# Modulation vectors: partition sums by VectorE with a 32x32 turn, and gate rows spread by repeating loads from DRAM

## The chip, the cores and the metric

The kernel runs on one core of a Trainium2 chip. The metric is the device time of one execution in microseconds (us). A core has five engines that run their own instruction streams side by side and wait for each other by semaphores: TensorE (PE in the profile, its weight loads PEld), VectorE (DVE), ScalarE (ACT), GpSimd (POOL) and SyncE (SP), which here mainly issues DMA transfers.

## The reference

One layer for 256 context rows and 2048 latent rows of width 1024. Two vectors (one for context rows, one for latent rows) go through a linear map and give six vectors of 1024 each, the modulation:

```python
def adaln(cvec, w_mod, b_mod):
    m = jax.nn.silu(cvec) @ w_mod + b_mod
    return jnp.split(m[:, None, :], 6, axis=-1)

sh1, sc1, g1, sh2, sc2, g2 = adaln(c, w_mod[l], b_mod[l])      # the same for c_ctx
h = rms_norm(xs, norm1_g[l]) * (1 + sc1) + sh1
q, k, v, f = project(h, w_in[l], q_norm_g[l], k_norm_g[l])     # one product, RMS norm of q and k
...                                                            # attention, Fourier mixing, w_out
xs = xs + g1 * mix
h = rms_norm(xs, norm2_g[l]) * (1 + sc2) + sh2
xs = xs + g2 * sq_relu_mlp(h, w1[l], w2[l])
```

The gates g1 and g2 multiply whole rows: each of the 1024 columns has its own factor, the same for all rows of a kind.

## The kernel before

The 2304 rows are 18 tiles of 128 rows; the context tiles and the latent tiles go through the same stages, one after the other: projection (to about 480 us), Fourier mixing (to about 600), attention, output projection (from about 1285), the first MLP product, the last product (from 2227 to the end).

**Projection.** `proj(i, g)` makes group g (0 to 3: q, k, v, Fourier) of tile i: 24 matmuls of 128x512 into one PSUM bank `pj{i}_{g}`, of which there are four in rotation. Each product is made of three, of high and low halves (lines 87 to 89). For q and k, ScalarE squares the bank (`sq{i}_0`, `sq{i}_1`, L250), VectorE sums the squares (`qss`, L251) and scales them (L254), GpSimd raises them to the power −1/2 (`qrs`, L255), and VectorE multiplies the bank by that (`qn`, L268). After that multiplication the bank is free for the next tile. The rotation of axial positions follows on VectorE (`qo`, `qt`, lines 293 to 303), then a transpose on TensorE (`ptqT`, `ptkT`, for the last tiles `ptqkT`, L310). The Fourier group is read by two operations of `f_post` on VectorE (`fo`, L387, and `fh`, L388); only then is its bank free.

The tiles 1 to 16 are one loop whose instructions a scheduler orders on each engine; tile 17 and all that follows is in an order written by hand. The engines keep the order that results, so an instruction that waits holds up all behind it on its engine.

**Modulation.** The weights of the modulation come in pieces of 1024x512 (a group; 12 in all). Groups 4 to 11 are made inside the loop, one in each odd turn i: SP loads the piece (`wm`), and `mod_group_v` accumulates on VectorE, for either of the two vectors, eight multiples of [128x512] tiles into `macc` (L164, L166). What is left is the sum over the 128 partitions. TensorE does it: eight fp32 matmuls of a 128x128 block of `macc` with a column of ones give `pm`, 128 results in 128 partitions each (L168), and a VectorE addition of the bias puts them into `modc` (L142), which holds the modulation with the column index in the partitions.

**Gates.** The multiplication by a gate needs its 1024 values along a row, the same in all 128 partitions. `mk_gate` makes half of such a tile: four fp32 matmuls take a column of `modc`, repeated 128 times, against the identity (`pg`, L180), and ScalarE copies the result (L181). It is called four times for `g1` in the output projection and four times for `g2` in the first turn of the last stage.

Of the kernel before, what the change touches and what calls it, by code (L numbers as in the profile page):

```python
# [11 lines left out]
F32 = mybir.dt.float32  # L12
F32R = mybir.dt.float32r
AF = mybir.ActivationFunctionType
ALU = mybir.AluOpType
AX = mybir.AxisListType
# [3 lines left out]
P = 128  # L20
D = 1024
# [20 lines left out]
def body(tc, a, out):  # L42
    nc = tc.nc
    ctx = ExitStack()
    with ctx:
# [6 lines left out]
        def scratch(name, shape):  # L52
            return dram.tile(shape, F32, tag=name, name=name)
# [9 lines left out]
        four = scratch("four", [512, NT])  # L63
        xnew = [scratch(f"xnew{i}", [P, D]) for i in range(NT // P)]
        HB = NT // 2
        hop = [[scratch(f"hd{p}_{b}", [P, 4, 384]) for b in range(3)] for p in range(8)]
        tsum = [scratch(f"tsum{k}", [P, 3, 512]) for k in range(16)]
        sop = [[scratch(f"sd{p}_{b}", [P, 16, 384]) for b in range(3)] for p in range(8)]

        ident = cst("ident", [P, P])  # L70
# [3 lines left out]
        ones = cst("ones", [P, 1])  # L74
# [65 lines left out]
        def mod_bias(gi, pm):  # L140
            b = cols[:, 32 + gi * 4:32 + gi * 4 + 4].unsqueeze(2).to_broadcast([P, 4, 2])
            nc.vector.tensor_add(modc[:, gi * 4:gi * 4 + 4, :], pm, b)  # L142
# [10 lines left out]
                nc.tensor.transpose(pm[:, j, :], r[0:2, j * P:(j + 1) * P], ident[0:2, 0:2])  # L153
            mod_bias(gi, pm)

        def mod_group_v(t2, pps, gi, w):

            pm = pps.tile([P, 4, 2], F32, tag="pm", name=f"pm{gi}")
            for s in range(2):
                acc = t2(f"macc{gi}_{s}")  # L160
                for k in range(KD):
                    wk, sc = w[k // 2][:, k % 2, :], cols[:, 8 * s + k:8 * s + k + 1]
                    if k == 0:
                        nc.vector.tensor_scalar_mul(acc, wk, sc)  # L164
                    else:
                        nc.vector.scalar_tensor_tensor(acc, wk, sc, acc, op0=ALU.mult, op1=ALU.add)  # L166
                for j in range(4):
                    nc.tensor.matmul(pm[:, j, s:s + 1], acc[:, j * P:(j + 1) * P], ones, start=True, stop=True)  # L168
            mod_bias(gi, pm)

        def mk_scale(dst, c0, gcol):
            nc.vector.tensor_scalar_add(dst, modc[:, c0:c0 + KD, :], 1.0)
            nc.vector.tensor_mul(dst, dst, cols[:, gcol:gcol + KD].unsqueeze(2).to_broadcast([P, KD, 2]))

        def mk_gate(pps, dst, c0, s, halves=(0, 1)):
            for hf in halves:
                pg = pps.tile([P, 512], F32, tag="pg", name=f"pg{c0}_{s}_{hf}", bufs=1)
                for j in range(4):
                    col = modc[:, c0 + hf * 4 + j, s:s + 1]
                    nc.tensor.matmul(pg[:, j * P:(j + 1) * P], col.to_broadcast([P, P]), ident, start=True, stop=True)  # L180
                nc.scalar.copy(dst[:, hf * 512:hf * 512 + 512], pg)  # L181

        def norm(pool, xt, nm, dst=None):

# [24 lines left out]
        with ExitStack() as c1:  # L209
# [6 lines left out]
            def t2(nm):  # L216
                return p1.tile([P, 512], F32, tag="t2", name=nm, bufs=6)
# [198 lines left out]
            with tc.manual_schedule():  # L416
# [108 lines left out]
                v_split(1, 0, vo0, "v0")  # L525
                load(3)
            wm, LAST = None, N1 - 1
            for i in range(1, LAST):
                mg = 3 + (i + 1) // 2
                if i >= 2 + N1 // 2 - 1:  # L530
                    f_load(i)
                    if i > 2 + N1 // 2 - 1:
                        f_rev(i - 1)
                if i % 2 and mg < 12:
                    wm = mod_load(po, mg)
                if i > 1:
                    norm(p1, X[i + 1], f"a{i + 1}")
                    proj(i, 0)
                transposed(i + 1)
                if 1 < i < N1 - 2:  # L540
                    load(i + 2)
                squares(i, 0)
                if i > 1:
                    proj(i, 1)
                qk_T(i - 1)
                squares(i, 1)
                proj(i, 2)
                qk_post(i)
                v_post(i)
                proj(i, 3)  # L550
                f_post(i)
                if i % 2 and mg < 12:
                    mod_group_v(t2, pps, mg, wm)
                if i in (4, 6, 8, 10):
                    cache_tile((i - 4) // 2)
            mk_scale(scale2, 32, 88)
# [853 lines left out]
        with c3o, ExitStack() as c4, ExitStack() as c4x, ExitStack() as c4w:  # L1410
# [22 lines left out]
            def x_load(i):  # L1433
                src = a["x_prompt"][0][i * P:i * P + P] if i < 2 else a["x_sample"][0][i * P - NP:i * P - NP + P]
                if i == LAST:
                    XT[i] = [f32(ms2s.tile([P, 2, 384], F32R, tag="sh", name=f"xo{i}_{hf}", bufs=2)).rearrange("p a b -> p (a b)")[:, 0:512]
                             for hf in range(2)]
                    for hf in range(2):
                        nc.sync.dma_start(XT[i][hf], src[:, hf * 512:hf * 512 + 512])
                else:  # L1440
                    XT[i] = tx.tile([P, D], F32, tag="x", name=f"xo{i}", bufs=3)
                    nc.sync.dma_start(XT[i], src)
# [73 lines left out]
            with tc.manual_schedule():  # L1516
                N4 = len(seq)
                s0, s1, s2 = seq[:3]
                mix_load(s1)
                x_load(s0)  # L1520
                x_load(s1)
                w_split(1, 0, 1)
                mix(s0)
                w_split(1, 1, 4)
                out_mm(s0, 1, 0, 2)
                for fn in LASTO[:2]:
                    fn()
                w_split(1, 4)
                out_mm(s0, 1, 2, 4)
                for fn in LASTO[2:]:  # L1530
                    fn()
                mix(s1)
                out_mm(s0, 1, 4)
                mk_gate(pp, g1[1], 16, 1, (1,))
                w_split(0)
                kv_even.close()
                ms1 = ctx.enter_context(tc.tile_pool(name="m_s1", bufs=2, side="right"))
                ms2s = ctx.enter_context(tc.tile_pool(name="m_s2s", bufs=2, side="right", reuse_waits="tile"))
                mix_load(s2)
                x_load(s2)  # L1540
                out_mm(s1, 1)
                mk_gate(pp, g1[0], 16, 0, (1,))
                out_post(s0, 1)
                out_mm(s0, 0)
                mk_gate(pp, g1[1], 16, 1, (0,))
                out_post(s1, 1)
                mix(s2)
                out_post(s0, 0)
                x_store(s0)
                x_norm(s0)  # L1550
                mix_load(seq[3])
                x_load(seq[3])
                out_mm(s1, 0)
                mk_gate(pp, g1[0], 16, 0, (0,))
                out_post(s1, 0)
                x_store(s1)
                x_norm(s1)
                finish(s0)
                for n, i in enumerate(seq[2:], 2):
                    out_mm(i, 0)  # L1560
                    if n < N4 - 1:
                        mix(seq[n + 1])
                    if n < N4 - 2:
                        mix_load(seq[n + 2])
                        x_load(seq[n + 2])
                    if n == N4 - 1:
                        c4w.close()
                        c4x.close()
                        ms2 = ctx.enter_context(tc.tile_pool(name="m_s2", bufs=2, side="right", reuse_waits="tile"))
                        c5r = ExitStack()  # L1570
                        hpa = c5r.enter_context(tc.tile_pool(name="m_ha", bufs=1, side="right", reuse_waits="tile"))
                    if n == N4 - 1:
                        mlp_ahead(0)
                    out_post(i, 0)
                    if n == N4 - 1:
                        mlp_ahead(3)
                    finish(seq[n - 1])
                    out_mm(i, 1)
                    if n == N4 - 1:
                        mlp_ahead(1)  # L1580
                    out_post(i, 1)
                    x_store(i)
                    if n < N4 - 1:
                        x_norm(i)
                    if n == N4 - 7:
                        w_load(0)
                    if n in (N4 - 6, N4 - 5, N4 - 4):
                        h_load(0, ORDER[n - N4 + 6])
                    if n == N4 - 3:
                        w_ahead()  # L1590
                        w_load(1)
# [250 lines left out]
        with ExitStack() as c6:  # L1842
# [62 lines left out]
            with tc.manual_schedule():  # L1905
                pend, NM, loaded, KS = None, 7 * 24, 4, []
                for i in range(7):
                    for b in range(3):
                        ps = [pp.tile([P, 512], F32, tag="ps", name=f"ps{i}_{b}_{j}", bufs=6) for j in range(3)]
                        for k in range(16):  # L1910
# [19 lines left out]
                            if (i, b) == (6, 2) and 9 <= k < 12:  # L1930
# [2 lines left out]
                                u = U3[6 + j]  # L1933
                                nc.vector.tensor_mul(u, u, g2[0][:, 0:512])
                                nc.vector.tensor_add(u, u, X[j])
                            if i == 0 and b == 1 and k in (2, 6, 10, 14):
                                s, hf = divmod(k // 4, 2)
                                mk_gate(pp, g2[s], 40, s, (hf,))
                            KS.append((k, SO[m], TO[n]))
                            if i == 6 and b == 2 and 12 <= k < 15:  # L1940
                                continue
# [84 lines left out]
```

## Time and profile before

| | |
|---|---|
| time, median of 3 runs (lowest, highest) | 2917.53 us (2917.14, 2917.74) |
| profiled execution: span from the first to the last instruction | 2919.2 us |
| TensorE busy | 2884.2 us, 99% |
| VectorE, ScalarE, GpSimd busy | 2018.9, 1564.1, 1044.6 us |
| mean granted TensorE clock | 0.998 |
| `pm` matmuls (L168) | 128 records, 107.3 to 456.2 us |
| `pg` matmuls (L180) | 64 records, 1293.5 to 2284.1 us |

The profiled execution has no other time of its own than its span, which is 1.7 us above the median of the timed runs. A row of a timeline gives start, duration, engine, line, operation, output <- inputs, shapes and count, and in brackets the idle time of the engine just before it with what ended it. A row of a window gives its length, then the busy time of PE, PEld, DVE, ACT and POOL with the number of instructions, the granted clock of TensorE (1.00 is full speed), the DMA share and GB/s. A row of the waits gives who waited for whom, the total, the number of waits and the longest.

### The profile page before, as it was taken

What the parts mean: (1) busy time and instruction counts of PE and PEld (TensorE: products, weight loads), DVE (VectorE), ACT (ScalarE), POOL (GpSimd) and SP (SyncE); (2) the same over time, 40 slices, a digit from 0 to 9 for tenths busy, and PEclk for the clock granted to TensorE, in tenths of its full rate; (3) what the DMA queues carried; (4) which work ended last, traced back from release to release, by engine and by line L of the source; (5) the groups of instructions that cost most, each with busy time, mean ns of one, the idle gap of its engine ahead of it and who ended that gap; (6) DMA issues with size and microseconds to landing.
All of it is one profiled execution on the core that took longest, in us unless ns stands there. A gap on an engine that the chain in (4) does not pass through costs nothing.

```text
span 2919.2 us, 43814 instructions
## 1 busy us (share of the span) xinstructions
PE 2884.2 (99%) x15425; PEld 2505.5 (86%) x15425; DVE 2018.9 (69%) x3401; ACT 1564.1 (54%) x3524; POOL 1044.6 (36%) x849
## 2 busy tenths in 40 slices
PE   8999999999999999999999999999999999999999
PEld 4888888688888888888889999999998888888887
DVE  6666777888998988964468778778775344345554
ACT  4333323688998989964356566556554322232221
POOL 1111113199898999952213333333332000000000
PEclk9999999999999999999999999999999999999999
DMA  7777878611121201217776677676656354445663
GB/s 280 198 203 189 224 199 254 230 67 71 44 104 47 109 28 46 89 54 214 215 247 214 221 238 234 221 239 221 222 189 235 124 197 153 135 142 174 205 206 108
DMA packets 394415, 495.59 MB, mean 170 GB/s; under 512 B 26403, under 2 KB 307056, under 8 KB 391122
## 3 DMA queue, kind: packets, MB, share of 16 engines
q1 hardware_dynamic: 386560, 477.63, 51.3%
q0 software_dynamic: 2992, 7.28, 0.8%
q10 hardware_dynamic: 4642, 7.88, 0.8%
q8 instruction: 122, 2.00, 0.3%
q14 instruction: 99, 0.81, 0.1%
HBM read 315.20 MB, written 179.57 MB: 169 GB/s over the span
## 4 chain that ended last, share of the span: by engine, by line
PE 91%; DMA 3%; ACT 2%; DVE 2%; issue 1%; POOL 1%; SPq 0%; ACTq 0%; POOLq 0%; DVEq 0%
PE Ss L969 10%; PE ps L87 8%; PE ps L88 8%; PE ps L89 8%; PE pts L1024 5%; PE pj L89 4%; PE pj L87 4%; PE pj L88 4%; PE po L89 4%; PE po L87 4%; PE po L88 4%; PE pA L1634 2%; PE pA L1635 2%; PE pB L1634 2%; PE pB L1635 2%; PE pB L1636 2%
## 5 line engine op out<-in xcount | busy, mean ns | idle before, releaser
L974 DVE TENSOR_REDUCE mxs<-Ss 128x1 f32<-128x512 f32 x636 | 413.2, 685 | 65.5 <-PE Ss L969 52.7
L1309 DVE TENSOR_TENSOR sl<-sr,sh 128x768 fp32r<-128x768 f32 x168 | 161.7, 964 | 340.0 <-ACT sh L1308 339.5
L1009 POOL TENSOR_TENSOR P0s<-P0s,P1s 128x1024 f32<-128x1024 f32 (+2 forms) x128 | 377.2, 2947 | 10.7
L1308 ACT CAST sh<-sr 128x768 fp32r<-128x768 f32 x168 | 140.1, 835 | 424.9 <-PE ps L88 424.9
L1676 POOL TENSOR_TENSOR gs<-g,g 128x384 f32<-128x384 f32 x48 | 69.7, 1452 | 469.6 <-ACT g L1646 400.9
L993 ACT ACTIVATE P1s<-Ss,mxs 128x512 f32<-128x512 f32 x318 | 215.4, 695 | 35.6 <-DVE mxs L977 34.2
L87 PE MATMUL pj<-wh,hh 128*128 128x512 f32 x576 | 229.5, 399 | 0.7 <-ACT fo L381 0.7
L88 PE MATMUL ps<-tlT,sh 128*128 128x512 f32 x585 | 229.3, 392 | 0.0
L87 PE MATMUL ps<-thT,sh 128*128 128x512 f32 x585 | 229.2, 392 | 0.0
L88 PE MATMUL pj<-wl,hh 128*128 128x512 f32 x576 | 227.7, 395 | 0.5 <-DVE wl L503 0.5
L89 PE MATMUL ps<-thT,sl 128*128 128x512 f32 x585 | 227.7, 389 | 0.0
L89 PE MATMUL pj<-wh,hl 128*128 128x512 f32 x576 | 226.7, 394 | 0.0
L993 ACT ACTIVATE P0s<-Ss,mxs 128x512 f32<-128x512 f32 x318 | 214.3, 691 | 4.3 <-DVE mxs L977 3.7
L969 PE MATMUL Ss<-KS1s,Qs 128*128 128x512 f32 x636 | 196.3, 420 | 5.7 <-ACT P0s L993 3.1
L969 PE MATMUL Ss<-KS0s,Qs 128*128 128x512 f32 x636 | 196.5, 421 | 2.4 <-ACT P1s L993 2.4
L1024 PEld LDWEIGHTS pts<-ident,P0s 128*128 128x128 f32 x1280 | 158.2, 140 | 42.9 <-ACT ahs L1031 3.1
L1024 PE MATMUL pts<-ident,P0s 128*128 128x128 f32 x1280 | 191.2, 273 | 0.7 <-ACT P1s L993 0.7
L1645 ACT ACTIVATE g<-uz 128x384 f32<-128x384 f32 x144 | 75.8, 527 | 201.0 <-DVE uz L1668 175.0
L1008 POOL TENSOR_SCALAR P1s<-P1s,tots 128x1024 f32<-128x1024 f32 (+2 forms) x128 | 172.1, 1345 | 5.7
L1036 DVE TENSOR_TENSOR als<-pts,ahs 128x512 fp32r<-128x512 f32 x256 | 165.8, 681 | 6.9 <-ACT ahs L1031 6.6
L87 PE MATMUL ps<-ophT,sh 128*128 128x512 f32 x423 | 165.9, 392 | 1.1 <-DVE uz L1668 1.1
L89 PE MATMUL ps<-ophT,sl 128*128 128x512 f32 x423 | 165.7, 392 | 0.0
(640 smaller groups left out, 8202.4 us busy)
## 6 DMA issues: line engine op xcount, KB each, us to landing
sr<-sd SPq DMA_DIRECT2D x84, 768.0 KB, 4.5
a<-in_w SPq DMA_DIRECT2D x184, 256.0 KB, 4.3
sd<-gs SPq DMA_DIRECT2D x192, 192.0 KB, 2.0
sd<-g SPq DMA_DIRECT2D x144, 192.0 KB, 4.4
wm<-in_w_mod SPq DMA_DIRECT2D x32, 512.0 KB, 5.8
Qs<-qd SPq DMA_DIRECT2D x32, 512.0 KB, 3.4
b<-in_w SPq DMA_DIRECT2D x64, 256.0 KB, 5.1
b<-tsum SPq DMA_DIRECT2D x64, 256.0 KB, 4.7
```

Source lines behind the costliest of these rows:

```text
L87: nc.tensor.matmul(ps, lh, rh, start=first, stop=False)
L88: nc.tensor.matmul(ps, lh, rl, start=False, stop=False)
L89: nc.tensor.matmul(ps, ll, rh, start=False, stop=last)
L969: nc.tensor.matmul(S[:, :w], self.Q[:, x, m, j * P:j * P + P], self.hd.KS[m][:, b * 512:b * 512 + w], start=(x == 0), stop=(x == 1))
L974: nc.vector.tensor_reduce(self.mx[j][:, m, b:b + 1], self.S[j, m, b], axis=AX.X, op=ALU.max)
L993: nc.scalar.activation(dst, S, AF.Exp, bias=self.mx[j][:, m, 6:7], accum_out=self.sm[j][:, m, b:b + 1])
L1008: nc.gpsimd.tensor_scalar(p, p, tot[:, 3:4], 0.0, op0=ALU.mult, op1=ALU.add)
L1009: nc.gpsimd.tensor_add(d, d, p)
L1024: nc.tensor.transpose(pt[:, c:c + P], self.p0[j][:, (kb + t) * P:(kb + t + 1) * P], ident)
L1036: nc.vector.tensor_sub(t, self.pt[kb], f32(self.A[kb][0]))
L1308: nc.scalar.copy(hi, src)
L1309: nc.vector.tensor_sub(lo, src, f32(hi))
```

## The change

The sum over partitions moves to VectorE. A `tensor_reduce` with `apply_transpose` turns each 32x32 block of `macc` and sums along it, which gives the sums over four bands of 32 partitions (`sums`). Once for four groups (after group 7 and after group 11), `mod_finish` adds up the four bands: GpSimd builds an operand `quad` from four pieces of the identity, and four fp32 matmuls with it give all results of four groups (`pm4`, `pm8`), to which one VectorE addition adds the bias. `gate_store` then turns the sixteen columns of `modc` that hold a gate into rows by a transpose on TensorE (`pgate0`, `pgate1`), ScalarE copies them (`gr0`, `gr1`), and SP writes them to DRAM. `mk_gate` and its calls are gone; `gate_load` fills a gate tile by a DMA that reads the row of 4 KB once for each partition.

```diff
-        def mod_group_v(t2, pps, gi, w):
-
-            pm = pps.tile([P, 4, 2], F32, tag="pm", name=f"pm{gi}")
+        def mod_group_v(t2, sums, gi, w):
+
             for s in range(2):
                 acc = t2(f"macc{gi}_{s}")
...
-                for j in range(4):
-                    nc.tensor.matmul(pm[:, j, s:s + 1], acc[:, j * P:(j + 1) * P], ones, start=True, stop=True)
-            mod_bias(gi, pm)
+                nc.vector.tensor_reduce(sums[:, gi % 4, s, :], acc.rearrange("p (c i) -> p c i", i=32), axis=AX.X, op=ALU.add,
+                                        apply_transpose=True)
+
+        def mod_finish(t2, pps, sums, gi):
+
+            z = t2(f"quad{gi}")[:, 0:224]
+            nc.gpsimd.memset(z, 0.0)
+            nc.gpsimd.tensor_add(z[:, 96:128], ident[:, 0:32], ident[:, 32:64])
+            for q in (2, 3):
+                nc.gpsimd.tensor_add(z[:, 96:128], z[:, 96:128], ident[:, 32 * q:32 * q + 32])
+            pm = pps.tile([P, 4, 2, 4], F32, tag="pm", name=f"pm{gi}")
+            for q in range(4):
+                nc.tensor.matmul(pm, z[:, 96 - 32 * q:224 - 32 * q], sums[:, :, :, q::4], start=(q == 0), stop=(q == 3))
+            nc.vector.tensor_add(modc[:, gi * 4:gi * 4 + 16, :].rearrange("p (g j) s -> p g j s", j=4), pm.rearrange("p g s j -> p g j s"),
+                                 cols[:, 32 + gi * 4:48 + gi * 4].rearrange("p (g j) -> p g j", j=4).unsqueeze(3).to_broadcast([P, 4, 4, 2]))
+
+        def gate_store(t2, pps, n):
+            c0 = (16, 40)[n]
+            pr = pps.tile([P, 512], F32, tag="pg", name=f"pgate{n}")
+            gr = t2(f"gr{n}")
+            nc.tensor.transpose(pr[0:16, 0:P], modc[:, c0:c0 + 8, :].rearrange("p k s -> p (k s)"), ident)
+            nc.scalar.copy(gr[0:16, 0:P], pr[0:16, 0:P])
+            for s in range(2):
+                nc.sync.dma_start(gates[n][s].rearrange("(k p) -> k p", p=P), gr[s:16:2, 0:P])
+
+        def gate_load(dst, n, s):
+            nc.sync.dma_start(dst, gates[n][s:s + 1, :].partition_broadcast(P).rearrange("p o d -> p (o d)"))
...
-        def mk_gate(pps, dst, c0, s, halves=(0, 1)):
...
                 if i % 2 and mg < 12:
-                    mod_group_v(t2, pps, mg, wm)
+                    mod_group_v(t2, sums, mg, wm)
+                    if mg % 4 == 3:
+                        mod_finish(t2, pps, sums, mg - 3)
+                        gate_store(t2, pps, mg // 8)
...
                 x_load(s0)
                 x_load(s1)
+                for s in (1, 0):
+                    gate_load(g1[s], 0, s)
...
-                mk_gate(pp, g1[1], 16, 1, (1,))
...
-                            if i == 0 and b == 1 and k in (2, 6, 10, 14):
-                                s, hf = divmod(k // 4, 2)
-                                mk_gate(pp, g2[s], 40, s, (hf,))
+                            if i == 0 and b == 1 and k in (2, 10):
+                                gate_load(g2[k // 8], 1, k // 8)
```

The lines of the projection stand 16 further down in the changed kernel (L250 is L266, L268 is L284, L87 is L88). The scheduler orders the loop anew, and three pieces of its order follow.

ScalarE around the squares of tile 8, before (first piece) and after (second); `sq8_0` and `sq8_1` are the squares, `hTa9` the normalised rows of tile 9, `nsqa11` the norm of tile 11, `kT7h` and `qT7h` copies of tile 7, `vo8` and `fo8` the banks of tile 8's groups 2 and 3:

```order
L250 ACTIVATE sq8_0_2385<-pj8_0_2333 128x512
L203 ACTIVATE hTa9_2358<-pta9_0_2359,modc_182,scale1_183 128x128 x4
L203 ACTIVATE hTa9_2358<-pta9_1_2368,modc_182,scale1_183 128x128 x4
L187 ACTIVATE nsqa11_2799,nssa11_2800<-x11_2618 128x1024
L250 ACTIVATE sq8_1_2443<-pj8_1_2388 128x512
L313 CAST kT7h_2418<-ptkT7_2413 128x512
L313 CAST qT7h_2431<-ptqT7_2426 128x512
L356 COPY vo8_2495<-pj8_2_2448 128x512
```

```order
L219 ACTIVATE hTa9_2346<-pta9_0_2347,modc_184,scale1_185 128x128 x4
L219 ACTIVATE hTa9_2346<-pta9_1_2356,modc_184,scale1_185 128x128 x4
L203 ACTIVATE nsqa11_2779,nssa11_2780<-x11_2606 128x1024
L329 CAST kT7h_2406<-ptkT7_2401 128x512
L329 CAST qT7h_2419<-ptqT7_2414 128x512
L188 COPY gr0_2309<-pgate0_2308 16x128
L266 ACTIVATE sq8_0_2373<-pj8_0_2321 128x512
L266 ACTIVATE sq8_1_2431<-pj8_1_2376 128x512
L372 COPY vo8_2483<-pj8_2_2436 128x512
```

The squares have moved behind `gr0`, the copy of the turned gate columns.

TensorE at the end of tile 8's last product (`pj8_3`), before and after; `macc7` are the accumulated multiples of group 7, `quad4` GpSimd's operand, `pj9_0` the first product of tile 9. Before, the 24 matmuls of `pj8_3` go on behind `pm7` and `pj9_0` follows them:

```order
L89 MATMUL pj8_3_2504<-wh3_2_355,hl8_2144 128x512
L168 MATMUL pm7_2298<-ones_180,macc7_0_2299 128x1 x4
L168 MATMUL pm7_2298<-ones_180,macc7_1_2312 128x1 x4
L87 MATMUL pj8_3_2504<-wh3_3_356,hh8_2143 128x512
L88 MATMUL pj8_3_2504<-wl3_3_364,hh8_2143 128x512
```

```order
L88 MATMUL pj8_3_2492<-wh3_7_362,hh8_2122 128x512
L89 MATMUL pj8_3_2492<-wl3_7_370,hh8_2122 128x512
L90 MATMUL pj8_3_2492<-wh3_7_362,hl8_2123 128x512
L179 MATMUL pm4_2302<-sums_768,quad4_2297 128x32 x4
L187 MATMUL pgate0_2308<-ident_175,modc_184 16x128
L88 MATMUL pj9_0_2558<-wh0_0_339,hh9_2365 128x512
```

The partition sums of groups 4 to 7 and the transpose of the first gate now stand between the two tiles.

VectorE around the last two tiles, before and after; `fo16`, `fh16` and `fo17`, `fh17` read the banks of group 3 of tiles 16 and 17, `v16l` is the low half of tile 16's group 2, and the last `qo16_1` is what the transpose `ptqkT16_1` on TensorE needs, which stands directly behind `pj17_3` in both kernels:

```order
L293 TENSOR_TENSOR qo16_1_4358<-qn16_1_4356,tb16_1_4359 128x512
L301 TENSOR_TENSOR qt16_1_4362<-qn16_1_4356,tb16_1_4359 128x8x32 x2
L347 TENSOR_TENSOR v16l_4370<-vo16_4366,v16h_4369 128x512
L303 TENSOR_TENSOR qo16_1_4358<-qo16_1_4358,qt16_1_4362 128x512
L387 TENSOR_TENSOR fo16_4400<-fh16_4196,pj16_3_4375 128x512
L388 TENSOR_TENSOR fh16_4196<-fh16_4196,pj16_3_4375 128x512
L387 TENSOR_TENSOR fo17_4439<-fh17_4411,pj17_3_4414 128x512
L388 TENSOR_TENSOR fh17_4411<-fh17_4411,pj17_3_4414 128x512
```

```order
L270 TENSOR_SCALAR qss16_4227<-qss16_4227 128x16
L284 TENSOR_TENSOR qn16_0_4319<-pj16_0_4179,qrs16_4228 128x512
L309 TENSOR_TENSOR qo16_0_4321<-qn16_0_4319,tb16_0_4322 128x512
L317 TENSOR_TENSOR qt16_0_4325<-qn16_0_4319,tb16_0_4322 128x8x32 x2
L284 TENSOR_TENSOR qn16_1_4329<-pj16_1_4232,qrs16_4228 128x512
L403 TENSOR_TENSOR fo17_4412<-fh17_4384,pj17_3_4387 128x512
L319 TENSOR_TENSOR qo16_0_4321<-qo16_0_4321,qt16_0_4325 128x512
L309 TENSOR_TENSOR qo16_1_4331<-qn16_1_4329,tb16_1_4332 128x512
L317 TENSOR_TENSOR qt16_1_4335<-qn16_1_4329,tb16_1_4332 128x8x32 x2
L404 TENSOR_TENSOR fh17_4384<-fh17_4384,pj17_3_4387 128x512
L363 TENSOR_TENSOR v16l_4343<-vo16_4339,v16h_4342 128x512
L319 TENSOR_TENSOR qo16_1_4331<-qo16_1_4331,qt16_1_4335 128x512
```

Before, all of tile 16's q and k stands ahead of `fo16`; now `fo16` and `fh16` come first, and the whole q chain of tile 16 stands behind them and around tile 17's `fo17` and `fh17`. In the same region of the other queues, `pgate1` stands on TensorE between `pj16_3` and `pj17_3`, and `gr1` on ScalarE ahead of `sq16_0`.

More of the change, by code (lines that the diff above doesn't have):

```diff
@@ L65, in body @@
         HB = NT // 2
+        gates = [scratch(f"gate{n}", [2, D]) for n in range(2)]
         hop = [[scratch(f"hd{p}_{b}", [P, 4, 384]) for b in range(3)] for p in range(8)]
@@ L173, in mk_scale @@
             nc.vector.tensor_mul(dst, dst, cols[:, gcol:gcol + KD].unsqueeze(2).to_broadcast([P, KD, 2]))
-        def mk_gate(pps, dst, c0, s, halves=(0, 1)):
[L176 to L181, printed above, removed]
         def norm(pool, xt, nm, dst=None):
@@ L527, in body @@
             wm, LAST = None, N1 - 1
+            sums = po.tile([P, 4, 2, 16], F32, tag="sums", name="sums", bufs=1)
             for i in range(1, LAST):
@@ L1541, in body @@
                 out_mm(s1, 1)
-                mk_gate(pp, g1[0], 16, 0, (1,))
                 out_post(s0, 1)
                 out_mm(s0, 0)
-                mk_gate(pp, g1[1], 16, 1, (0,))
                 out_post(s1, 1)
@@ L1553, in body @@
                 out_mm(s1, 0)
-                mk_gate(pp, g1[0], 16, 0, (0,))
                 out_post(s1, 0)
```

## The prediction

> **What bounds the kernel now.** I read the busy table first, then the chain that ended last, then the stretches in which the change works (windows), then TensorE's waits there.
>
> ```profile
> PE 2884.2 (99%) x15425; PEld 2505.5 (86%) x15425; DVE 2018.9 (69%) x3401; ACT 1564.1 (54%) x3524; POOL 1044.6 (36%) x849
> PE 91%; DMA 3%; ACT 2%; DVE 2%; issue 1%; POOL 1%; SPq 0%; ACTq 0%; POOLq 0%; DVEq 0%
> ```
> ```profile
> 90.00:470.00 380.00, 380.00 (x1862) 316.74 (x1861) 263.06 (x485) 118.30 (x255) 57.72 (x28) 1.00 0.77 202
> ```
> ```profile
> PE rev L755 <- DVE d L741: 2.0, 1, 2.0
> PE py L88 <- DVE able L697: 1.6, 1, 1.6
> ```
>
> TensorE (PE) is busy 99% of the span and makes up 91% of the last chain. In the projection, 90 to 470 us, where the change does most, it is busy 380 of 380 us at full clock (1.00), with VectorE at 263 and ScalarE at 118. From 60 to 560 us its two longest waits are 2.0 and 1.6 us, both behind the projection. So a TensorE instruction that goes is time saved, and a TensorE wait that comes is time lost; nothing else gives either back. The forecast weighs the one against the other.
>
> **What goes from TensorE.** The small matmuls lie between large ones:
>
> ```profile
> 107.05 0.39 PE L88 MATMUL pj<-wl,hh 128*128 128x512 f32 x1
> 107.28 1.84 PE L168 MATMUL pm<-ones,macc 128*128 128x1 f32 x16
> 108.98 0.48 PE L89 MATMUL pj<-wh,hl 128*128 128x512 f32 x1
> ```
> ```profile
> 2255.65 0.40 PE L89 MATMUL ps<-ophT,sl 128*128 128x512 f32 x1
> 2255.89 1.05 PE L180 MATMUL pg<-ident,modc 128*128 128x128 f32 x8
> 2256.70 0.48 PE L87 MATMUL ps<-ophT,sh 128*128 128x512 f32 x1
> ```
>
> The block of 16 records holds its place from 107.28 to 108.98, 1.70 us, and the matmul behind it takes 0.48 instead of 0.39: 1.79 a block, eight blocks in tiles 2 to 16, **−14.3**. A gate block of eight records pushes the next matmul from the usual 0.23 (213.68 to 213.91 below) to 1.05 behind the one before (0.82), and it takes 0.48 for 0.40: 0.90. Four stand in the last stage where TensorE is never idle, **−3.6**. Of the four in the out-projection three pull all behind them forward, **−2.7**. The fourth is followed by a wait:
>
> ```profile
> 1314.91 1.09 PE L200 MATMUL ptb<-ident,xn 128*128 128x128 f32 x8 [0.63 <-DVE xn L191]
> ```
>
> TensorE already waits 0.63 us there for the norm of the row tile, so the fourth buys more waiting: 0.
>
> **What comes to VectorE and GpSimd.** Sixteen reduces of 128x512 with the turn, which no row shows. The lower bound is the plain reduce of the same size, 0.68; the upper takes a pass over the tile (0.477, L164) ahead of it, 1.15. I take 0.68, as the same number of elements is read once.
>
> ```profile
> L251 DVE TENSOR_REDUCE qss<-sq x36: 671/681/687, 67.5 to 480.3; 128x8 f32<-128x512 f32 x36
> L164 DVE TENSOR_SCALAR macc<-wm,cols x16: 474/477/480, 87.3 to 434.9; 128x512 f32<-128x512 f32 x16
> ```
>
> [...] On VectorE alone (263 of 380 us busy) 11 us more cost nothing, and POOL (58 of 380) makes the two `quad` operands, a memset and three adds of 128x32 each, ahead of time; they count where they stand ahead of what TensorE waits for. That is the q chain of a tile: squares (ACT), `qss` (VectorE), the scale of it (L254), the power on POOL, `qn` (L268). `qn` frees the PSUM bank that the next tile's first product needs. The order of the changed kernel puts both reduces ahead of the scale at tiles 6 and 10, and behind it (under the power's 2.9 us) at 12 and 14; tiles 2 and 4 I take as covered, since `qn` has more in hand there. Tiles 6 and 10 before:
>
> ```profile
> 211.36 0.69 DVE L268 TENSOR_TENSOR qn<-pj,qrs 128x512 f32<-128x512 f32 x1 [3.09 <-POOL qrs L255]
> 310.93 0.69 DVE L268 TENSOR_TENSOR qn<-pj,qrs 128x512 f32<-128x512 f32 x1 [3.09 <-POOL qrs L255]
> ```
> ```profile
> 213.68 0.39 PE L89 MATMUL pj<-wh,hl 128*128 128x512 f32 x1
> 213.91 0.39 PE L87 MATMUL pj<-wh,hh 128*128 128x512 f32 x1
> ...
> 313.46 0.39 PE L87 MATMUL pj<-wh,hh 128*128 128x512 f32 x1
> ```
>
> `qn` ends at 212.05 and 311.62; the next tile begins at 213.91 and 313.46: 1.85 us in hand. TensorE now comes 1.80 earlier (no `pm`), `qn` 1.2 later (two reduces at a step of 0.60, as VectorE steps below): 1.8 + 1.2 − 1.85, some 1.2 us of new wait at each, **+2.4**.
>
> **What stalls TensorE: tile 8.** ScalarE's order now has `gr0` (the copy of the turned gates) ahead of both squares of tile 8, and TensorE has `pm4` and `pgate0` behind tile 8's last product. So the whole q chain waits for that product, and tile 9 for the chain:
>
> ```profile
> L250 ACT ACTIVATE sq<-pj x36: 577/598/618, 66.6 to 479.5; 128x512 f32<-128x512 f32 x36
> ```
> ```profile
> 257.64 0.16 DVE L254 TENSOR_SCALAR qss<-qss 128x16 f32<-128x16 f32 x1
> 257.95 2.91 POOL L255 TENSOR_TENSOR qrs<-qss,mhalf 128x16 f32<-128x16 f32 x1 [4.25 <-DVE qss L254]
> 260.89 0.69 DVE L268 TENSOR_TENSOR qn<-pj,qrs 128x512 f32<-128x512 f32 x1 [3.09 <-POOL qrs L255]
> ```
>
> From the product's end: four matmuls `pm4` 0.98 (eight records, 0.115 each by the L168 row above, 1.84 over 16, or 0.13 by the L180 row, 1.05 over 8: 0.92 to 1.05); the add 0.16 and its handoffs, to 1.3; `pgate0` 0.27, to 1.6; `gr0` of 128 columns 0.3 (half a square's 0.60), to 1.9; two squares at 0.50, the second ending at 2.95; the second `qss` 0.68 and handoffs, to 3.8; scale 0.16, to 3.95; 0.15 handoff and 2.91, to 7.0; `qn` 0.69, to 7.75. Tile 9 begins 7.8 us after tile 8's product, 1.25 of it in new records and the rest idle, where before it followed at once: **+7.8**. The stall also costs clock:
>
> ```profile
> 518.48 1.39 PE L755 MATMUL rev<-d,jm 128*128 128x512 f32 x2 [2.01 <-DVE d L741]
> ```
> ```profile
> 519.00:520.00 1.00, 1.00 (x3) 0.56 (x2) 1.00 (x3) 0.00 (x0) 0.00 (x0) 0.57 1.11 297
> 520.00:521.00 1.00, 1.00 (x3) 0.34 (x2) 0.80 (x2) 0.00 (x0) 0.00 (x0) 0.50 1.04 252
> 521.00:522.00 1.00, 1.00 (x4) 0.63 (x3) 0.00 (x0) 0.00 (x0) 0.00 (x0) 0.50 0.91 186
> 522.00:523.00 1.00, 1.00 (x9) 1.00 (x8) 0.00 (x0) 0.18 (x1) 0.00 (x0) 0.72 0.60 111
> ```
>
> Behind the idle of 2.01 us the granted clock is 0.57, 0.50, 0.50, 0.72: 0.43 + 0.50 + 0.50 + 0.28 = 1.7 us lost. Tile 8 gets the same: **+1.7**, 9.5 in all. A shorter idle did not do it:
>
> ```profile
> 536.73 0.39 PE L88 MATMUL py<-able,cwh 128*128 128x256 f32 x1 [1.58 <-DVE able L697]
> ```
> ```profile
> 538.00:540.00 2.00, 2.00 (x17) 1.76 (x16) 2.00 (x5) 1.27 (x4) 0.00 (x0) 1.00 0.00 0
> ```
>
> So the limit lies between 1.6 and 2.0 here, and the waits of 1.2 at tiles 6 and 10 and of 1.4 at tile 17 below stay under it. [...]
>
> **Tiles 16 and 17.** `pm8` stands inside tile 16's last product: +0.94. `pgate1` stands behind that product, then tile 17's group 3, whose bank is tile 16's, freed by the second of two VectorE operations:
>
> ```profile
> 467.59 0.69 DVE L387 TENSOR_TENSOR fo<-fh,pj 128x512 f32<-128x512 f32 x1 [3.82 <-PE pj L89]
> 468.31 0.69 DVE L388 TENSOR_TENSOR fh<-fh,pj 128x512 f32<-128x512 f32 x1
> ```
>
> 0.72 + 0.69 and two handoffs: **+1.66**, of which 1.4 idle. Then the same trap as at tile 8: `gr1` ahead of tile 16's squares. Counted from the end of tile 16's product: `pgate1` and `gr1` 0.65, squares to 1.75, `qss` and scale to 2.75, power to 5.75, handoff to 5.9. Then VectorE runs from `qn16_0` to the last `qo16_1`, written in that order: eleven places at its steps of
>
> ```profile
> 458.02 0.76 DVE L301 TENSOR_TENSOR qt<-qn,tb 128x256 f32<-128x256 f32 x2
> 458.69 0.69 DVE L268 TENSOR_TENSOR qn<-pj,qrs 128x512 f32<-128x512 f32 x1
> 459.29 0.68 DVE L303 TENSOR_TENSOR qo<-qo,qt 128x512 f32<-128x512 f32 x1
> ```
>
> 0.67 (a pair `qt`) and 0.60: 9 x 0.60 + 2 x 0.67 + 0.1 = 6.85, to 12.9 with the handoff. TensorE ends tile 17's group 3 at 1.66 + 24 x 0.23 = 7.2 and then wants `ptqkT16_1`, which needs that `qo16_1`: **+5.7** idle. Before, the same transposes followed the product at once. A clock spell again, **+1.7**. Sum of the place 0.94 + 1.66 + 5.7 + 1.7 = **+10.0**.
>
> **What the later idle takes back.** The wait at 518.48 is released through VectorE by DMAs, and the chain of waits goes back to
>
> ```profile
> 500.61 10.20 DMA vd<-v17l
> ```
>
> The loads of the Fourier tables and SP's queue do not all depend on TensorE; if they keep their times while TensorE comes some 5 us later, the 2.01 idle and its 1.65 of clock go. If all were fed by TensorE, nothing goes. Half: **−1.8** (0 to −3.7).
>
> **Gate loads.** Each is 512 KB from SP; the rows for that size are
>
> ```profile
> wm<-in_w_mod SPq DMA_DIRECT2D x32, 512.0 KB, 5.8
> ```
> ```profile
> L1481 DVE TENSOR_TENSOR gt<-po,g x36: 681/684/692, 1300.5 to 1513.7; 128x512 f32<-128x512 f32 x36
> ```
>
> The first multiply by a gate starts at 1300.5; the loads are issued behind `x_load(s1)`, and two of them take 11.6 us at worst. The stage's own tiles must be loaded, merged and multiplied before that multiply as well, so I take the gates as there. They went to DRAM at tile 8, a thousand us before; those of the last stage, first used at its end, have more room still. The four issues on SP push later loads by about 0.5 us each: 0. If SP is held up there, `mix_load(s2)` comes late (below, the late gate load).
>
> **Sum.** −14.3 − 3.6 − 2.7 + 2.4 + 9.5 + 10.0 − 1.8 = −0.5. The profiled span is 2919.2, 1.7 above the median of the runs shown, 2917.53; the difference is applied to the median: **2917.0 us**, no change. Anything within 0.2% (5.8 us) is what a measurement of this kernel can hardly tell from none.
>
> **The rivals.**
> *The clock stays at half longer (slower).* After another idle of 2.17 us the clock was still half four to six microseconds later:
>
> ```profile
> 38.04 1.97 PE L494 MATMUL pta<-ident,x 128*128 128x128 f32 x8 [2.17 <-DVE hTa L479]
> ```
> ```profile
> 42.00:44.00 2.00, 2.00 (x6) 1.61 (x5) 2.00 (x5) 2.00 (x6) 0.00 (x0) 0.50 0.57 193
> ```
>
> Six microseconds at half cost 3.0 instead of 1.7, +1.3 at each of the two spells; if the 1.4 us idle ahead of tile 17 drops it too, a third one, +3.0; and if the wait at 518 is not shortened, +1.8. Together +7.4: 2924.4. It decides when both spells last 6 us and a third occurs (+5.6), or the later wait stays. Against it: TensorE was badly fed from 38 to 44, and is fed without a break behind these stalls. A dearer reduce (1.15) adds 0.5 for each that stands ahead of a scale, four to six of them, another +2 to +3. Chance 0.32.
> *The stalls are shorter (faster).* The clock does not fall (−3.4), the whole late idle goes (−1.9), the reduces cost no wait at 6 and 10 (−2.4): −7.7, 2909.3. It decides from −5.4 on, so nearly all of it must hold. For it: my chains add every handoff; against: the 2.01 us row. Chance 0.24.
> *A gate load comes late.* If SP's queue holds at the broadcast load, each tile load behind it moves by up to 5.8 us, of which some 3 would reach TensorE in the out-projection: 2920. Part of no change, 0.04.
> *It does not do what it says.* If the copies `gr` come earlier than ordered, no stall at all: −20 and more. The order is fixed at build time, so 0.01 inside the faster chance.
>
> **How the numbers follow.** No change, 0.44 (the sum 0.40, late loads 0.04); slower 0.32; faster 0.24. The range reaches from the faster case less 2 (handoffs shorter by 1 in each chain), 2907, to the slower one with dear reduces (+2.5) and part of a late load, 2929.
>
> **What would show it.** Right: no L168 or L180 rows; TensorE waits of about 6.5 us at tile 9's first product (released by `qn`) and 5.7 at `ptqkT16_1` (by `qo`), with clock 0.5 for some 3 us behind both; waits of about 1.2 at tiles 7 and 11; reduces of 0.68. Wrong: no wait over 3 us in the projection (then 2909 or less), or clock spells of 6 us and more, or waits of TensorE in the out-projection that point to a gate or a tile load (then slower).

## The result and the profile after

The changed kernel takes 2920.34 us (median of 12 runs, 2918.07 to 2922.75), the kernel before 2918.72 (12 runs beside it). The ratio is 1.0006, 95% interval 0.9998 to 1.0014: no change that can be told. The forecast was 2917.0, no change, and the time lies in its range.

The page of the changed kernel, busy time and last chain, then the window of the projection:

```profile
PE 2868.8 (98%) x15251; PEld 2488.5 (85%) x15251; DVE 2029.0 (69%) x3411; ACT 1560.5 (53%) x3518; POOL 1051.6 (36%) x857
PE 89%; DVE 4%; ACT 3%; DMA 2%; POOL 1%; issue 1%; SPq 0%; ACTq 0%; DVEq 0%; POOLq 0%
```
```profile
90.00:470.00 380.00, 368.79 (x1736) 303.93 (x1735) 265.97 (x483) 117.72 (x255) 63.01 (x36) 0.99 0.77 199
```

TensorE is busy 15 us less, yet the span is 1.7 us longer (2920.9 for 2919.2). In the projection it was busy 380 of 380 us, now 368.79, and the clock is no longer 1.00. What was taken from TensorE has come back as waiting. TensorE's waits from 60 to 560 us, the longest six:

```profile
PE pj L88 <- DVE qn L284: 9.5, 4, 6.2
PE ptqkT L326 <- DVE qo L319: 5.7, 1, 5.7
PE py L89 <- DVE able L717: 1.5, 1, 1.5
PE pj L88 <- DVE fh L404: 1.4, 1, 1.4
PE rev L775 <- DVE d L761: 1.3, 1, 1.3
PE pj L88 <- ACT fo L397: 0.7, 1, 0.7
```

The first, second and fourth are new. Tile 8 on TensorE, ScalarE and VectorE (three timelines):

```profile
257.92 0.98 PE L179 MATMUL pm<-sums,quad 128*128 128x32 f32 x8
259.18 0.28 PE L187 MATMUL pgate<-ident,modc 128*16 128x128 f32 x1 [0.28 <-DVE modc L180]
265.62 0.76 PE L88 MATMUL pj<-wh,hh 128*128 128x512 f32 x1 [6.16 <-DVE qn L284]
```
```profile
259.49 0.26 ACT L188 COPY gr<-pgate 16x128 f32<-16x128 f32 x1 [10.49 <-PE pgate L187]
259.65 1.06 ACT L266 ACTIVATE sq<-pj 128x512 f32<-128x512 f32 x2
```
```profile
258.93 0.19 DVE L180 TENSOR_TENSOR modc<-pm,cols 128x32 f32<-128x32 f32 x1 [3.70 <-PE pm L179]
260.27 1.28 DVE L267 TENSOR_REDUCE qss<-sq 128x8 f32<-128x512 f32 x2 [1.15 <-ACT sq L266]
264.78 0.69 DVE L284 TENSOR_TENSOR qn<-pj,qrs 128x512 f32<-128x512 f32 x1 [3.02 <-POOL qrs L271]
```

ScalarE sits idle for 10.49 us before the small copy `gr`, with both squares behind it; VectorE waits for `pm4`. Tile 9 begins 7.70 us after the last product of tile 8. The clock behind it, in steps of two microseconds:

```profile
264.00:266.00 2.00, 0.38 (x1) 0.41 (x2) 1.19 (x2) 0.00 (x0) 0.75 (x1) 0.50 0.27 103
266.00:268.00 2.00, 2.00 (x6) 1.52 (x6) 2.00 (x6) 0.00 (x0) 0.00 (x0) 0.50 0.08 17
268.00:270.00 2.00, 2.00 (x6) 1.54 (x5) 2.00 (x6) 0.62 (x1) 0.00 (x0) 0.50 0.65 202
270.00:272.00 2.00, 2.00 (x7) 1.58 (x6) 0.95 (x3) 0.00 (x0) 0.00 (x0) 0.67 0.93 276
```

It is half until about 271, some 5.5 us from the start of tile 9. Tiles 16 and 17:

```profile
463.06 0.27 PE L187 MATMUL pgate<-ident,modc 128*16 128x128 f32 x1
464.72 0.50 PE L88 MATMUL pj<-wh,hh 128*128 128x512 f32 x1 [1.39 <-DVE fh L404]
476.20 1.94 PE L326 MATMUL ptqkT<-ident,qo 128*128 128x128 f32 x8 [5.70 <-DVE qo L319]
```

Where the changed kernel stands against the one before, by the start of the same instruction in the two traces (the multiplies by g2 are VectorE's, all else is TensorE's):

| place | before, us | after, us | after less before |
|---|---|---|---|
| tile 2, second group | 101.12 | 101.29 | +0.2 |
| tile 8, last product, first matmul | 256.39 | 252.42 | −4.0 |
| tile 9, second group | 269.18 | 273.85 | +4.7 |
| tile 16, third group, last matmul | 454.37 | 456.43 | +2.1 |
| Fourier stage, first product | 484.8 | 495.5 | +10.7 |
| attention, first scores | 558.9 | 567.2 | +8.3 |
| attention, last transpose | 1282.7 | 1290.8 | +8.1 |
| MLP, first product | 1513.5 | 1519.1 | +5.6 |
| MLP, last matmul into `pA` | 2208.5 | 2213.9 | +5.4 |
| first multiply by g2 (L1882; L1900 in the changed kernel) | 2357.3 | 2359.1 | +1.8 |
| last multiply by g2 in that line | 2892.2 | 2894.0 | +1.8 |

So the gains and losses are nearly as large as forecast, and they cancel.

### The profile page after: what moved, and what is told of

Its sections match the earlier page's. It is cut to its first block, busy times and chain, and to the rows that moved or that the text cites. A ratio compares the mean times of both kernels' runs of the same rounds, so it can differ in the third digit from the quotient of the medians.

```text
span 2920.9 us, 43514 instructions
## 1 busy us (share of the span) xinstructions
PE 2868.8 (98%) x15251; PEld 2488.5 (85%) x15251; DVE 2029.0 (69%) x3411; ACT 1560.5 (53%) x3518; POOL 1051.6 (36%) x857
## 4 chain that ended last, share of the span: by engine, by line
PE 89%; DVE 4%; ACT 3%; DMA 2%; POOL 1%; issue 1%; SPq 0%; ACTq 0%; DVEq 0%; POOLq 0%
PE Ss L989 10%; PE ps L88 8%; PE ps L89 8%; PE ps L90 8%; PE pts L1044 5%; PE po L90 4%; PE po L88 4%; PE pj L88 4%; PE po L89 4%; PE pj L89 4%; PE pj L90 4%; PE pA L1652 2%; PE pA L1653 2%; PE pB L1653 2%; PE pB L1652 2%; PE pB L1654 2%
## 5 line engine op out<-in xcount | busy, mean ns | idle before, releaser
L1029 POOL TENSOR_TENSOR P0s<-P0s,P1s 128x1024 f32<-128x1024 f32 (+2 forms) x128 | 377.1, 2946 | 10.7
L88 PE MATMUL pj<-wh,hh 128*128 128x512 f32 x576 | 231.5, 402 | 11.6 <-DVE qn L284 9.5
L88 PE MATMUL ps<-thT,sh 128*128 128x512 f32 x585 | 229.0, 391 | 0.0
L88 PE MATMUL ps<-ophT,sh 128*128 128x512 f32 x423 | 165.7, 392 | 1.1 <-DVE uz L1686 1.1
```

The costliest lines, as they stand in the source:

```text
L88: nc.tensor.matmul(ps, lh, rh, start=first, stop=False)
L1029: nc.gpsimd.tensor_add(d, d, p)
```

## The experiments

The kernel before was run again beside the experiments: 2917.12 us beside the first four, 2918.47 beside the other four. Numbers of the two groups are compared by their distance from it.

**Theory 1:** the small copies `gr0` and `gr1` and the turns they wait for, ordered ahead of the squares, make both long stalls. **Theory 2:** the stalls come from `pm4` and `pm8` and the addition that waits for them. The first experiment moves only `gate_store`, out of the loop into the part ordered by hand.

```diff
                     if mg % 4 == 3:
                         mod_finish(t2, pps, sums, mg - 3)
-                        gate_store(t2, pps, mg // 8)
...
                 squares(LAST, 1, True)
+                gate_store(t2, pps, 0, "pm")
+                gate_store(t2, pps, 1, "pg")
```

(The last argument names the PSUM tile; `pm` is made as large as `pg` for that.)

> Only the two gate_store steps (turn on TensorE, copy on ScalarE, DMA to DRAM) move, out of the loop into the hand-written part behind the squares of tile 17; the sums by VectorE and mod_finish stay in the loop. Theory 1 (the copies gr0 and gr1 ahead of the squares on ScalarE make both long stalls): the idle of 6.2 us before tile 9 and of 5.7 us before ptqkT16_1 are gone, each under 1 us, no half clock there; -9.5 at tile 8 and -9.3 at tiles 16/17 (pm4 and pm8 stay), +0.5 for the two turns, and some +2.4 that the wait near 518 us takes back: about 2904.5. Theory 2 (the partition-sum matmuls pm4 and pm8 and the VectorE addition that waits for them hold the q chain): the stalls stay at 4 to 5 us each, 2914 to 2917.

Measured: 2906.44 us against 2917.12 of the kernel before beside it, ratio 0.9961 (0.9948 to 0.9973). It beats both kernels. TensorE's waits from 60 to 560 us, the two longest and `rev`:

```profile
PE pz L88 <- DVE ys L704: 3.1, 1, 3.1
PE pj L88 <- DVE qn L284: 1.7, 2, 1.3
...
PE rev L776 <- DVE d L762: 0.6, 1, 0.6
```

The waits of 6.2 and 5.7 are gone while `pm4` and `pm8` are still in the loop, `pm4` at 257.18 us. Theory 2 falls. The time is 2 us above the number of theory 1. (The profile is of the fastest of the five runs, 2903.08 us, with no half clock from 60 us on.)

The second leaves the first `gate_store` at tile 8 and moves only the other:

```diff
-                        gate_store(t2, pps, mg // 8)
+                        if mg == 7:
+                            gate_store(t2, pps, 0, "pg")
...
                 squares(LAST, 1, True)
+                gate_store(t2, pps, 1, "pg")
```

> Only the second gate_store (after group 11) moves to the hand-written part; the first stays at tile 8. Theory 1: tile 8 as in the changed kernel (7.7 us from the product's end to tile 9, and 2.7 us of half clock), no stall before ptqkT16_1; the wait near 518 us shorter, as TensorE comes late there: 2911 to 2914. Theory 2: both stalls as in the changed kernel or a little less, 2916 to 2920. The half clock: if it is set by the length of the idle time, the spell behind tile 8 is again 5 to 6 us long; if by chance, it changes.

Measured: 2913.67, ratio 0.9988 (0.9979 to 0.9997), 7.2 above e_store. The stall at tile 8 is there as before (`qn`, longest 6.2), none before `ptqkT`. The spell of half clock was shorter behind the same idle time of 6.16 us: tile 9's first group took 7.56 us here (264.05 to 271.61), 8.23 in the changed kernel (265.62 to 273.85) and 5.49 in the kernel before (263.69 to 269.18), so 2.1 us were lost instead of 2.7. The idle time alone does not set the spell's length.

```profile
PE pj L88 <- DVE qn L284: 9.3, 4, 6.2
```

The next two part the change's two halves. Gates by the old matmuls, everything else as in e_store:

```diff
-                gate_store(t2, pps, 0, "pm")
-                gate_store(t2, pps, 1, "pg")
...
-                    gate_load(g1[s], 0, s)
...
+                mk_gate(pp, g1[1], 16, 1, (1,))
```

> As e_store, but without any gate rows in DRAM: gates by the old matmuls (mk_gate) in the output projection and the last stage. If the gate matmuls are worth their place on TensorE (0.9 us each, seven of eight counted) and the two turns cost 0.5, this is 5.8 us above e_store, about 2910. Rival (the gate loads cost elsewhere what the matmuls give, by DMA time or SP's queue): less than 3 us above e_store.

Measured: 2910.76, ratio 0.9978 (0.9969 to 0.9987), 4.3 above e_store: between the two expectations. Gate rows through DRAM pay, if less than the 5.8 worked out.

The sums by the old matmuls, the gates through DRAM:

```diff
                 squares(LAST, 1, True)
+                gate_store(t2, pps, 0, "pm")
+                gate_store(t2, pps, 1, "pg")
...
+                    gate_load(g1[s], 0, s)
...
-                mk_gate(pp, g1[1], 16, 1, (1,))
```

> The kernel before (sums over partitions by 8 small matmuls for 128 per group) with only the gate rows through DRAM, gate_store in the hand-written part. By the forecast's gate terms, -6.3 and +0.5 for the turns: 2912 to 2913 against 2918.7. Against e_store it gives what the sums by VectorE are worth without the stalls: eight blocks of 1.8 less 1.9 for pm4 and pm8 and less the waits of the reduces at tiles 6 and 10 to 14 (4.5 by the changed kernel's trace) would be 8 us above e_store; if the waits of the reduces eat the gain, it is equal to e_store.

Measured: 2913.62, ratio 0.9989 (0.9980 to 0.9998); 3.5 below the kernel before, 7.2 above e_store. So the sums by VectorE are worth 7 us where they cause no stall, and the 8 that were worked out are nearly right.

Is it ScalarE, or any engine of the chain? The changed kernel with the copies on VectorE:

```diff
-            nc.scalar.copy(gr[0:16, 0:P], pr[0:16, 0:P])
+            nc.vector.tensor_copy(gr[0:16, 0:P], pr[0:16, 0:P])
```

> The changed kernel with only the copies gr0 and gr1 moved from ScalarE to VectorE; the turns stay on TensorE between the tiles. ScalarE's squares of tile 8 now wait for nothing new, but on VectorE the addition of pm4's results and the copy gr0 stand ahead of the sums qss of these squares. Theory 1a (it is ScalarE's copy alone): no stall before tile 9, about 2908 to 2911. Theory 1b (any engine of the q chain that must first wait for the turn stalls the tile; ScalarE is only where the order put it): the two squares (1.1 us) leave the chain and the rest stays, some 5 us idle before tile 9 and 4.5 to 5.5 before ptqkT16_1: 2916 to 2919.

Measured: 2921.41, ratio 1.0012 (1.0003 to 1.0021).

```profile
PE pj L88 <- DVE qn L284: 8.0, 3, 5.6
PE ptqkT L326 <- DVE qo L319: 4.5, 1, 4.5
```

The waits are those of theory 1b, 5.6 and 4.5 us, though both squares of tile 8 now ran at 248.76 us, 11 us earlier. The time is 2 us above its range. The wait for `fh` before tile 17 rose from 1.4 to 2.0 us, and here the clock fell behind it:

```profile
463.18 0.50 PE L88 MATMUL pj<-wh,hh 128*128 128x512 f32 x1 [2.04 <-DVE fh L404]
```
```profile
464.00:466.00 2.00, 2.00 (x6) 1.59 (x5) 0.00 (x0) 1.02 (x2) 1.99 (x1) 0.50 0.36 133
```

That spell lasted from 464.0 to about 467.3, some 1.7 us lost, and the half clock behind `ptqkT` lasted longer too (5.9 us from its start, to about 481.0, against 3.3, to about 479.5, in the changed kernel). So the stalls stay whichever of the two engines copies; they go with the place of the turn between the tiles.

The e_store profile has a wait of 3.1 us for VectorE, which waits for loads that stand behind the gate stores in SP's queue. The next kernel stores the gates later still (the turn and its copy then use tiles of the Fourier stage):

```diff
-                gate_store(t2, pps, 0, "pm")
-                gate_store(t2, pps, 1, "pg")
                 c_load(1)
...
                         prep(3 if n == "p" else 1)
+                        if n == "f" and g < 2:
+                            gate_store(ft, pp, g)
```

> e_store with gate_store moved further on, into the Fourier stage's last part. In e_store TensorE waits 3.1 us at 505.8 us for VectorE, which waits for the loads of fsum; the kernels with gate_store ahead of those loads in SP's queue show that wait, the one without (e_pegate) does not. If the four gate stores on SP delay the loads, this wait goes and the time falls by 1 to 2 us against e_store (2904.5 to 2905.5); if the wait is the lead that TensorE gained, it stays and the time is that of e_store.

Measured: 2912.87 against 2918.47, ratio 0.9980 (0.9971 to 0.9988). It is 5.6 us under the kernel before, where e_store was 10.7 under it: some 5 us **worse**, against both expectations (the two intervals just touch), and the wait for `ys` is still 2.6. SP's queue in e_tail:

```profile
511.99 1.28 SPq L350 DMA_DIRECT2D qd<-qkT_0l  x2
536.21 2.86 SPq L190 DMA_DIRECT2D gate<-gr  x4
539.25 0.32 SPq L936 DMA_DIRECT2D KS0s<-kd  x1
539.61 0.43 SPq L936 DMA_DIRECT2D KS1s<-kd  x1
540.21 0.32 SPq L964 DMA_DIRECT2D Qs<-qd  x1
```

and in e_store:

```profile
515.21 0.33 SPq L936 DMA_DIRECT2D KS0s<-kd  x1
```

The gate stores wait for `gr` until 536.21, and the attention's loads of keys, which went at 515 in e_store, stand behind them. TensorE in e_tail then waits for these loads, the second time through ScalarE:

```profile
551.19 3.53 PE L990 MATMUL Ss<-KS0s,Qs 128*128 128x512 f32 x10 [1.84 <-DMA Qs<-qd]
568.87 2.07 PE L990 MATMUL Ss<-KS1s,Qs 128*128 128x512 f32 x4 [5.56 <-ACT P0s L1014]
```
```profile
568.04 0.69 ACT L1014 ACTIVATE P0s<-Ss,mxs 128x512 f32<-128x512 f32 x1 [5.52 <-DMA KS1p<-kd]
```

It is the same fault as at tile 8, on another engine's queue: a small instruction that waits long ahead of something urgent. In e_store the longest wait of TensorE in the first 17 us of the attention is 0.97 us. The gate stores do not make the wait for `ys`; what the 3.1 us in e_store come from stays open.

The reduces one turn later, on top of e_tail:

```diff
+                if i % 2 == 0 and mg < 12:
+                    mod_sum(sums, mg)
                     if mg % 4 == 3:
                         mod_finish(t2, pps, sums, mg - 3)
```

(`mod_sum` holds the two reduces that stood at the end of `mod_group_v`.)

> e_tail with the reduces of a group issued one turn of the loop later, which puts them behind the scale of qss at tiles 8 to 14 (under GpSimd's power). If the reduces ahead of the scale cost what the traces of the changed kernel and of e_store show as waits for qn (1.7 us in all in e_store), this is 1 to 2 us under e_tail; if they were hidden already, equal to it.

Measured: 2913.11, ratio 0.9981 (0.9972 to 0.9990), equal to e_tail. TensorE's waits for `qn` came to 1.4 us instead of 1.7, so the move took hardly any of them away, and nothing of it shows in the time.

The kernel before, profiled once more, without an edit:

> The kernel before, profiled a second time: is the wait of 2.0 us near 518 us followed by half clock again? If an idle of that length always costs the clock, yes, 1.7 us lost as before; if the drop there was a matter of phase (e_store idles 3.1 us at 505.8 at full clock), it can be absent.

Measured: 2915.08 (one run; the lowest of the 27 beside it is 2915.46). The wait was 0.73 us and no half clock followed:

```profile
516.42 1.10 PE L755 MATMUL rev<-d,jm 128*128 128x512 f32 x2 [0.73 <-DVE d L741]
```

## Why the prediction was right, term by term

| term of the sum | forecast | from the trace after |
|---|---|---|
| eight `pm` blocks | −14.3 | −14.5 (1.81 each at tiles 2 and 4) |
| waits behind the reduces, tiles 6 to 14 | +2.4 | +4.1 |
| tile 8 | +9.5 | +10.4 (gap 7.70, clock 2.7) |
| tiles 16 and 17 | +10.0 | +10.4 |
| up to the first scores | −1.8 | −2.4 |
| out-projection gates | −2.7 | −2.5 |
| last stage's gates | −3.6 | −3.6 |

The rows of the projection are the jumps of TensorE's lead between one product and the next, with 1.81 a block taken out. The first row is this 1.81 for all eight blocks. The terms of the last column add up to +1.9; the spans differ by 1.7, the medians by 1.6. The forecast has the place, the order of the steps and nearly the length of each stall. The idle before `ptqkT` is 5.70 us for the forecast 5.7; before tile 9 it is 6.16 for about 6.5. It came out because the chain was followed through the order of each engine and each step priced from a row. The fourth gate block of the out-projection bought only waiting, as forecast: the wait for `xn` rose from 0.63 to 1.48 us.

Two terms were mis-sized. *The waits behind the reduces* were forecast as 1.2 us at tiles 6 and 10 alone; the trace has TensorE waiting for `qn` 1.05 us before tile 7, 1.63 before tile 11 and 0.68 before tile 13, 3.4 in all; the rest of the 4.1 is some 0.25 us that each restart costs beyond its idle time (behind the 1.63 us the starts follow at 316.08, 318.11 and 318.45 us, where two steps of 0.23 are usual: 1.91 lost). The reduce itself was right: 

```profile
L167 DVE TRANSPOSE_TENSOR_REDUCE sums<-macc x16: 671/704/711, 107.2 to 453.8; 128x16 f32<-128x512 f32 x16
```

0.704 us, against 0.681 for the plain reduce: the turn costs next to nothing. *The clock behind tile 8* cost 2.7 us, not 1.7: it was half for 5.5 us, where some 3 were forecast. That there would be a spell at all rested on the row of 2.01 us, and behind idle times of about that length the clock held as often as it fell (of nineteen from 1.84 to 3.10 us it fell behind nine; last section); behind all seven of 4.26 us and more it fell.

The step on *the later idle* gave nearly its number: the wait fell from 2.01 to 1.28 us and its 1.7 us of clock went, 2.4 together. But its ground does not hold. In the second profile of the kernel before, the wait at 516 us is 0.73 us without half clock, so the 2.01 us and the spell behind it belong to one execution and not to the kernel. That the number fits is luck, and how much of the −2.4 the change caused is open. The step on the gate loads held: no wait for a gate in the output projection, and the e_pegate and e_gates runs put the gates' worth at 4.3 and 3.5 us.

Of the rivals, the longer half clock was partly there (2.7 at one place), without a spell behind the 1.39 us before tile 17. The faster rival needed the clock to hold behind both stalls, and it did not. That the change "does not do what it says" fell at the order: `gr` came where it stood.

## What to carry to other kernels

Here a few small operations taken from the bound engine came near their price (some 7 us of 8 for the sums, 4.3 of 5.8 for the gates) only where what replaced them wasn't put ahead of that engine's next input. Read in the order which instructions the new small ones precede on each engine and DMA queue (behind `gr0` ScalarE held two squares, with 10.49 us idle; in e_tail the loads of keys, issued at 515.21 us in e_store, stood in SP's queue until 539.25), and price the whole chain from where the small one can start. If that cancels the gain, move the small step to where nothing urgent stands behind it: here that turned 1.6 us above the kernel before into 10.7 under it, and the wrong place on SP's queue took some 5 of it back.

## What the runs showed of the hardware

Between 60 and 600 us the ten traces show seven idle times of TensorE from 4.26 to 6.16 us, and its clock fell to half behind each of them; it fell behind none of up to 1.74 us. In between, length does not decide. It fell behind 1.84 (e_tail) and 2.68 us (e_redlate), both ahead of the first scores, behind 2.01 (before) and 2.26 us (e_redlate) ahead of `rev`, and behind 2.04 us (e_vcopy) ahead of tile 17's last group. Behind 2.36, 2.60, 2.66 and 3.10 us ahead of `pz` it held.

The instruction does not decide either. At one place of the attention all ten traces have the same wait of 1.99 to 2.01 us; the clock fell behind it in four (before, after, e_pegate, e_tail) and held in six. Here are the kernel before and the same kernel in e_again, then the longest wait without half clock, in e_store:

```profile
590.10 0.74 PE L969 MATMUL Ss<-KS0s,Qs 128*128 128x512 f32 x2 [1.99 <-ACT P1s L993]
```
```profile
591.00:593.00 2.00, 2.00 (x7) 1.59 (x6) 1.10 (x2) 2.00 (x7) 1.92 (x2) 0.50 0.04 8
```
```profile
586.46 0.73 PE L969 MATMUL Ss<-KS0s,Qs 128*128 128x512 f32 x2 [2.01 <-ACT P1s L993]
```
```profile
587.00:589.00 2.00, 2.00 (x14) 1.69 (x13) 1.57 (x3) 2.00 (x8) 1.92 (x2) 1.00 0.02 6
```
```profile
505.78 0.50 PE L88 MATMUL pz<-abho,cwh 128*128 128x512 f32 x1 [3.10 <-DVE ys L704]
```
```profile
506.00:508.00 2.00, 2.00 (x16) 1.87 (x16) 2.00 (x4) 0.37 (x1) 0.00 (x0) 1.00 0.80 254
```

So behind some 2 us the same kernel can lose the clock in one execution and keep it in the next, and a spell seen in one profile, worth some 1.7 us, must not be booked to the kernel. The forecast's reading that a limit lies between 1.6 and 2.0 us was wrong: behind 3.10 us (e_store) the clock held. What decides there is not shown.
